# A YOCO trunk on one core: attention's pipeline started 4 modelled us later, and sixteen weight splits given to GpSimd

## Chip, core and metric

The kernel runs on one core of a Trainium2 chip. The metric is device time in microseconds (us), a median of runs. TensorE (PE in the profile; PEld is its weight load) multiplies, VectorE (DVE), ScalarE (ACT) and GpSimd (POOL) do the element-wise work, and SyncE (SP) issues most DMAs. Each engine works through its own queue in order.

## What is computed

Two layers over 1056 columns (a prompt of 1024 frames and a sample of 32), model width 1024. Layer 0 is an mLSTM mixer and a SwiGLU FFN, layer 1 a sliding-window attention and a SwiGLU FFN; each sub-layer ends in a layer norm of alpha * x + sublayer(x). The change lies in layer 1:

```python
kv = (x @ w_kv).reshape(B, T, 2, N_KV_HEADS, HEAD_DIM)
k_sh, v_sh = kv[:, :, 0], kv[:, :, 1]
...
s = jnp.einsum('bcqhgd,bckhd->bchgqk', q, k).astype(F32) * (HEAD_DIM ** -0.5) + bias
sk = sinks.astype(F32).reshape(N_KV_HEADS, GROUP)[:, :, None, None]
mx = jnp.maximum(jnp.max(s, -1, keepdims=True), sk)
p = jnp.exp(s - mx)
p = p / (jnp.sum(p, -1, keepdims=True) + jnp.exp(sk - mx))
return jnp.einsum('bchgqk,bckhd->bcqhgd', p.astype(v.dtype), v)
...
return o.reshape(B, T, D_ATT) @ w_out
```

## The kernel before

Activations lie transposed in SBUF: 128 partitions by 8 tiles of the width by 1056 columns. For projections the columns form three groups of 384, 384 and 288; for output projections and layer norms four quarters of 264. Every fp32 operand is split into a high and a low fp32r part, and each product is three matmuls, high by high, high by low and low by high (L361, L362, L363, in `gemm`). I call the three of one contraction tile a step; eight steps make an output tile.

**Weights.** The class `Weights` holds one list of units in the order of use, each 128x1024. SyncE loads a unit into one of three raw buffers `wr` (L160). A unit has two halves; for each, ScalarE copies the high part `wh` (L201) and VectorE or GpSimd subtracts to give the low part `wl` (L203). GpSimd does it unless the half is in the set `on_vector` (L314 adds output weights to it). Five slots hold split halves, and some units have homes elsewhere. `feed`, called from each step through `wv.tick`, makes the next split when a pause has passed; `mixer_out` also splits two tiles ahead in its first two quarters (`split_to`).

**Order.** `Weave` keeps generators beside the matmuls. A yielded number is a time in modelled us; each step ticks by its modelled length, and when a generator's time is up it emits its next instructions. So all queues are fixed when the program is built.

**Attention.** After layer 0, `keys_values(0)` makes keys and values of group 0 and the first four query tiles are projected. Then `v_turn` transposes the values of a group (L1668 on TensorE, L1622 and L1623 split them into `VR`; the output tag `O` has two banks, shared with the attention output), and `attention` is launched. It runs `pipeline` over 72 pairs of a two-head query tile j and a block b of 128 columns: scores (L1693, L1694 into one bank `psS` for each head, then bias and running reduction L1699 on VectorE), softmax (exponent L1711 on ScalarE, L1715 on VectorE, scaling L1717 on GpSimd), transposes of the probabilities into one bank `T` (L1737, read by L1740 on ScalarE and L1741 on VectorE, which frees it), values (L1752, L1753) and placing (L1761, L1763). Beside it run the key and value projections of groups 1 and 2 (units 108 and 109, twice), and then query projections (units 110 to 117); L1608 and L1609 on SyncE place a query tile. Later, `mixed_parts` splits attention's result (L391 on ScalarE, L392 on VectorE), and the output projection of the first quarter (units 118 to 125, `U_OUT_B[0]`, evicted at L1202) runs beside attention's last 15 steps or so. The other three quarters read the same weights again, as units 126 to 133, `U_OUT_B[1]`.

Of the kernel before, what the change touches and what calls it, by code (L numbers as in the profile page):

```python
# [101 lines left out]
def pipeline(seq, stages, order=None):  # L102


    n = [0] * len(stages)
    total = len(seq)

    def can(i):
        return n[i] < total and (i == 0 or n[i] < n[i - 1]) and stages[i][1](*seq[n[i]])

    while n[-1] < total:
        moved = False
        for i in order or range(len(stages)):
            work, _, lag, pause = stages[i]
            if not can(i) or (i + 1 < len(stages) and n[i] - n[i + 1] > stages[i + 1][2]):
                continue
            if i and n[i - 1] - n[i] <= lag and n[i - 1] < total:
                continue
            item = seq[n[i]]
            work(*item)  # L120
            n[i] += 1
            moved = True
            if pause:
                yield pause[item[0]]
        if not moved:
            yield 0.25
# [115 lines left out]
def kernel(ctx: ExitStack, tc: tile.TileContext, A, O):  # L242
# [23 lines left out]
    units, on_vector, pairs = [], set(), set()  # L266

    def add(name, idx):
        units.append(A[name][idx] if idx is not None else A[name])
        return len(units) - 1  # L270
# [15 lines left out]
    U_OUT_A = [[add("wout_a", m) for m in range(8)]] * 2  # L286
    U_UP, U_DN = [], []

    def add_ffn(layer):
        up, dn = {}, []  # L290
        for c, i in VISITS:
            held = up.get((i, 1 - c)) if i == FIRST - 1 else None
            up[i, c] = held or [add("gu", 2 * (layer * FT + i) + k) for k in range(2)]
        for i in range(FIRST, FT):
            up[i] = add_pair("gu", 2 * (layer * FT + i))
        for b in range(TAIL):
            dn.append([add_pair("dn", 4 * (layer * TAIL + b) + 2 * j) for j in range(2)])
        dn.append([add("dnt", KT * layer + m) for m in range(KT)])
        on_vector.update((u, 1) for u in dn[TAIL])
        on_vector.update((u, f) for i in range(FIRST) for c in range(2) for u in up[i, c] for f in range(2))  # L300
        U_UP.append(up)
        U_DN.append(dn)
# [8 lines left out]
    U_QB[0] += U_QB[1][4:]  # L311
    U_OUT_B = [[add("wout_b", u) for u in range(8)] for _ in range(2)]
    add_ffn(1)
    on_vector.update((u, f) for u in U_OUT_A[0] + U_OUT_B[0] + U_OUT_B[1] for f in range(2))  # L314
    on_vector.update((u, f) for u in U_Q[:1] for f in range(2))
    W = Weights(nc, base, units, pairs, on_vector)
    wv.feed = W.feed
# [1356 lines left out]
    def attention(gap):  # L1674
# [82 lines left out]
        def place(j, b):  # L1757
# [8 lines left out]
            ast["placed"] += 1  # L1766

        always = lambda j, b: True
        yield from pipeline(
            [(j, 3 * g + i) for j, g in QG for i in range(3)],  # L1770
            [
# [15 lines left out]
    wv.drain(placing)  # L1787
    wv.launch(v_turn(0, 0))
    task = wv.launch(attention((GAP_A,) * 8))
    ast["ready"] = 4  # L1790
    for g in range(1, 3):
# [179 lines left out]
```

## Time and profile before

| | us |
|---|---|
| median of 3 runs | 2244.7 (2244.04 to 2245.94) |
| the profiled execution | 2244.99 |
| its span on the core | 2242.9 |
| PE busy in the span | 2187.7 |
| DVE, ACT, POOL busy | 1472.7, 999.6, 1018.3 |

The span is the time from the profile's first instruction to its last; the rest of the execution lies around it. A row of a timeline has start, length, engine, line, operation, output and inputs by name (buffer numbers left out), shape and count, and in brackets the idle time ahead of it with what ended it. Matmul lengths overlap, so the time of one is read from start to start. A row of a stretch has bounds, length, busy time of each engine with its instructions, the granted TensorE clock (1.00 is full), the share of the DMA engines and GB/s. A row of a group ends in busy time and mean ns of one.

### The profile page before, as it was taken

To read this page: it belongs to the slowest core of one execution; us is meant where nothing else is said; L and a number is where in the kernel's file an instruction comes from. 1 tells how busy PE (TensorE), PEld (TensorE's weight loads), DVE (VectorE), ACT (ScalarE), POOL (GpSimd) and SP (SyncE) were. 2 spreads that over 40 slices of the span, in tenths; PEclk is the share of its full clock that TensorE was granted. 3 is DMA by queue.
4 is the path that set the end of the run, shared out by engine and by line. 5 is a ranking of instruction groups with operands and counts; after the bars stand their busy time and mean duration, and the time that the engine had idled before them with its cause. 6 is when DMAs were issued, how large, how long until landed. Compare 5 with 4: busy or idle time off the path is not lost.

```text
span 2242.9 us, 44249 instructions
## 1 busy us (share of the span) xinstructions
PE 2187.7 (98%) x17086; PEld 2151.6 (96%) x17086; DVE 1472.7 (66%) x2864; ACT 999.6 (45%) x2253; POOL 1018.3 (45%) x961
## 2 busy tenths in 40 slices
PE   9999999999999999999998999899999999999997
PEld 9899999999999999999998999899999999999997
DVE  4465576777566665566667678888666666456657
ACT  4443355465344444322246678656444444332124
POOL 2544331003665666545326676400566666554422
PEclk9999999999999999999999999999999999999999
DMA  4222112211443443697425433421344434397712
GB/s 149 75 54 69 53 40 86 96 39 58 165 138 140 154 152 137 230 332 232 153 79 169 115 99 95 138 78 39 106 154 160 139 134 154 135 347 242 257 50 78
DMA packets 174499, 298.10 MB, mean 133 GB/s; under 512 B 18065, under 2 KB 130761, under 8 KB 174289
## 3 DMA queue, kind: packets, MB, share of 16 engines
q1 hardware_dynamic: 169936, 290.94, 39.1%
q10 hardware_dynamic: 4352, 4.33, 0.6%
q8 instruction: 135, 2.21, 0.4%
q14 instruction: 76, 0.61, 0.1%
HBM read 201.80 MB, written 82.94 MB: 127 GB/s over the span
## 4 chain that ended last, share of the span: by engine, by line
PE 80%; DVE 8%; ACT 4%; DMA 3%; issue 3%; POOL 1%; SPq 0%; ACTq 0%; DVEq 0%; POOLq 0%
PE A L361 9%; PE A L363 9%; PE A L362 9%; PE d L361 8%; PE d L363 8%; PE d L362 8%; PE B L361 7%; PE B L362 7%; PE B L363 7%; PE T L1737 1%; DMA wr<-in_dn 1%; ACT act L463 1%; PE T L906 1%; PE O L1752 1%; DVE wl L203 1%
## 5 line engine op out<-in xcount | busy, mean ns | idle before, releaser
L203 POOL TENSOR_TENSOR wl_s<-wr,wh_s 128x512 fp32r<-128x512 f32 x224 | 316.6, 1434 | 243.0 <-ACT wh_s L201 182.6
L361 PE MATMUL d<-sx,wh 128*128 128x264 f32 (+2 forms) x1068 | 341.1, 319 | 0.7 <-DVE act L1525 0.7
L363 PE MATMUL d<-sx,wl 128*128 128x264 f32 (+2 forms) x1068 | 326.2, 305 | 1.4 <-POOL wl L203 1.4
L362 PE MATMUL d<-sx,wh 128*128 128x264 f32 (+2 forms) x1068 | 325.3, 305 | 0.1
L203 POOL TENSOR_TENSOR wl_a<-wr,wh_a 128x512 fp32r<-128x512 f32 x112 | 169.0, 1515 | 331.2 <-ACT wh_a L201 329.5
L201 ACT CAST wh_s<-wr 128x512 fp32r<-128x512 f32 x224 | 135.4, 617 | 310.9 <-DVE wr L178 279.4
L361 PE MATMUL A<-sx,wh_s 128*128 128x264 f32 x896 | 255.4, 285 | 3.5 <-ACT z L1358 3.5
L362 PE MATMUL A<-sx,wh_s 128*128 128x264 f32 x896 | 254.9, 284 | 0.0
L363 PE MATMUL A<-sx,wl_s 128*128 128x264 f32 x896 | 254.8, 284 | 0.0
L361 PEld LDWEIGHTS d<-sx,wh 128*128 128x128 f32 x1068 | 202.6, 190 | 4.3 <-ACT z L444 1.1
L363 PEld LDWEIGHTS d<-sx,wl 128*128 128x128 f32 x1068 | 201.6, 189 | 2.5 <-POOL wl L203 2.2
L362 PEld LDWEIGHTS d<-sx,wh 128*128 128x128 f32 x1068 | 202.3, 189 | 1.1 <-DVE sx L392 0.4
L363 PE MATMUL d<-sx,ex 128*128 128x264 f32 x624 | 177.7, 285 | 3.5 <-DVE ex L203 3.5
L361 PE MATMUL d<-sx,ex 128*128 128x264 f32 x624 | 180.6, 289 | 0.4 <-ACT sx L391 0.2
L203 POOL TENSOR_TENSOR wl<-wr,wh 128x512 fp32r<-128x512 f32 (+2 forms) x75 | 100.1, 1344 | 177.5 <-ACT wh L201 154.5
L362 PE MATMUL d<-sx,ex 128*128 128x264 f32 x624 | 177.3, 284 | 0.3 <-DVE sx L392 0.2
L361 PEld LDWEIGHTS A<-sx,wh_s 128*128 128x128 f32 x896 | 169.3, 189 | 4.0 <-ACT z L1358 4.0
L363 PEld LDWEIGHTS A<-sx,wl_s 128*128 128x128 f32 x896 | 169.6, 189 | 0.0
L362 PEld LDWEIGHTS A<-sx,wh_s 128*128 128x128 f32 x896 | 169.2, 189 | 0.0
L1270 POOL TENSOR_TENSOR z<-z 128x528 fp32r<-128x528 f32 x76 | 105.3, 1385 | 109.2 <-issue 58.0
L1717 POOL TENSOR_SCALAR s<-s,st 128x256 f32<-128x256 f32 (+1 forms) x144 | 126.6, 891 | 61.3 <-DVE st L1715 47.6
L1269 ACT CAST z<-z 128x528 fp32r<-128x528 f32 x136 | 85.9, 631 | 95.5 <-DVE z L1282 44.9
(338 smaller groups left out, 7299.3 us busy)
## 6 DMA issues: line engine op xcount, KB each, us to landing
wr<-in_gu SPq DMA_DIRECT2D x92, 512.0 KB, 4.9
hs_x<-z SPq DMA_DIRECT2D x72, 528.0 KB, 2.8
hs_t<-z SPq DMA_DIRECT2D x64, 528.0 KB, 2.9
sx<-hs_x SPq DMA_DIRECT2D x112, 264.0 KB, 5.9
sx<-hs_t SPq DMA_DIRECT2D x64, 264.0 KB, 6.4
ex<-hs_t SPq DMA_DIRECT2D x64, 264.0 KB, 6.4
wr<-in_dn SPq DMA_DIRECT2D x32, 512.0 KB, 3.9
ex<-hs_x SPq DMA_DIRECT2D x32, 264.0 KB, 5.9
```

Of the source, the lines that this page charges most:

```text
L201: self.nc.scalar.copy(hi, r)
L203: eng.tensor_sub(lo, r, hi.bitcast(F32))
L361: nc.tensor.matmul(out, ah, bh, start=start and k == 0, stop=False, **kw)
L362: nc.tensor.matmul(out, ah, bl, start=False, stop=False, **kw)
L363: nc.tensor.matmul(out, al, bh, start=False, stop=stop and k == last, **kw)
L463: nc.scalar.activation(z, z, AF.Identity, scale=gk, bias=bk)
L906: nc.tensor.matmul(pc[:, : 2 * (DV + 1)], keys, vt[j][:L, c], start=True, stop=True)
L1269: nc.scalar.copy(hi.bitcast(F32R), buf(s))
L1270: eng.tensor_sub(lo.bitcast(F32R), buf(s), hi)
L1717: nc.gpsimd.tensor_scalar_mul(p[:R, h, lo:256], p[:R, h, lo:256], st[:R, 2, h : h + 1])
L1737: nc.tensor.transpose(pt[:nk, i, h, :R], p[:R, h, c : c + nk], ident[:R, :R])
L1752: nc.tensor.matmul(po[:, :, :R], v, s["hi"][:nk, i, :, :R], start=(i == 0), stop=False)
```

## The change

`U_OUT_B[0]` leaves the set `on_vector`, so the low parts of the sixteen halves of units 118 to 125 are made by GpSimd. And the generator of `attention` yields 4.0 ahead of its pipeline.

```diff
-    on_vector.update((u, f) for u in U_OUT_A[0] + U_OUT_B[0] + U_OUT_B[1] for f in range(2))
+    on_vector.update((u, f) for u in U_OUT_A[0] + U_OUT_B[1] for f in range(2))
...
         always = lambda j, b: True
+        yield 4.0
         yield from pipeline(
```

On TensorE, at the start of attention (`d` is a projection, `O` here a transposed value tile, `psS` scores), before:

```order
L1668 MATMUL O_14303<-ident,act 128x128
L1693 MATMUL psS_13944<-KH_13946,Q_14111 128x128
L1694 MATMUL psS_13944<-KL_13948,Q_14111 128x128
L1693 MATMUL psS_13945<-KH_13946,Q_14111 128x128
L1694 MATMUL psS_13945<-KL_13948,Q_14111 128x128
L1693 MATMUL psS_13944<-KH_13946,Q_14111 128x256
```

And there in the changed kernel:

```order
L1668 MATMUL O_14303<-ident,act 128x128
L361 MATMUL d_14293<-sx,wh_0_14197 128x384
L362 MATMUL d_14293<-sx,wh_0_14197 128x384
L363 MATMUL d_14293<-sx,wl_0_14198 128x384
L1668 MATMUL O_14310<-ident,act 128x128
...
L1668 MATMUL O_14320<-ident,act 128x128
...
L361 MATMUL d_14342<-sx,wh_0_14261 128x384
L362 MATMUL d_14342<-sx,wh_0_14261 128x384
L363 MATMUL d_14342<-sx,wl_0_14262 128x384
L1693 MATMUL psS_13944<-KH_13946,Q_14111 128x128
```

Two blocks of scores stood right behind the first value transpose; now the rest of the key projection (`d_14293`), two more transposes and the first step of the value projection (`d_14342`) are ahead of the first scores. The twelve first attention steps move back in the same way, among the projections of group 2 and of the first queries; six value transposes now stand among them, three before. From the projection of unit 111 on, the order of TensorE is the old one.

On GpSimd, in the last part of attention (`wl` is the low part of a split, `s` the probabilities of one step):

```order
 L1717 TENSOR_SCALAR s_16964<-s_16964,st_16965 128x256 x2
+L203 TENSOR_TENSOR wl_1_17020<-wr_15495,wh_1_17019 128x512
 L1717 TENSOR_SCALAR s_17010<-s_17010,st_17011 128x256 x2
+L203 TENSOR_TENSOR wl_0_17083<-wr_15668,wh_0_17082 128x512
 L1717 TENSOR_SCALAR s_17056<-s_17056,st_17057 32x160 x2
 L1717 TENSOR_SCALAR s_17108<-s_17108,st_17109 128x256 x2
+L203 TENSOR_TENSOR wl_1_17166<-wr_15668,wh_1_17165 128x512
+L203 TENSOR_TENSOR wl_0_17172<-wr_16022,wh_0_17171 128x512
 L1717 TENSOR_SCALAR s_17150<-s_17150,st_17151 128x256 x2
 L1717 TENSOR_SCALAR s_17214<-s_17214,st_17215 128x256 x2
+L203 TENSOR_TENSOR wl_1_17274<-wr_16022,wh_1_17273 128x512
+L203 TENSOR_TENSOR wl_0_17280<-wr_17023,wh_0_17279 128x512
```

GpSimd had only scalings there; now two splits stand behind every second one. On VectorE the same splits leave a place just ahead of L1763 and L1741 (`act` is attention's result, `lo` the low part of the transposes `T`):

```order
 L1202 SCALAR_TENSOR_TENSOR act<-act,d_17175 128x264
-L203 TENSOR_TENSOR wl_1_17274<-wr_16022,wh_1_17273 128x512
-L203 TENSOR_TENSOR wl_0_17280<-wr_17023,wh_0_17279 128x512
 L1763 TENSOR_TENSOR act<-O_17246,t_17287 64x32 x2
 L1741 TENSOR_TENSOR lo_17293<-T_17291,hi_17292 128x512
```

The read of the transposes now follows the eviction of the output tile (L1202) and the placing alone.

## The prediction

> **What bounds the kernel now.** I read the page first, for what is busy and for the chain of work that ended last; then that chain in order of time over the attention stage; then the timeline of single engines at its waits.
>
> ```profile
> span 2242.9 us, 44249 instructions
> PE 2187.7 (98%) x17086; PEld 2151.6 (96%) x17086; DVE 1472.7 (66%) x2864; ACT 999.6 (45%) x2253; POOL 1018.3 (45%) x961
> PE 80%; DVE 8%; ACT 4%; DMA 3%; issue 3%; POOL 1%; SPq 0%; ACTq 0%; DVEq 0%; POOLq 0%
> 1216.80:1264.70 47.90, 41.26 (x280) 38.57 (x278) 30.76 (x112) 31.13 (x98) 35.17 (x46) 0.96 0.50 136
> 1394.00:1446.00 52.00, 44.14 (x349) 41.82 (x346) 44.88 (x152) 40.29 (x120) 29.30 (x30) 0.97 0.39 124
> ```
>
> TensorE sets the time. The last two rows are stretches (bounds, length, then busy time of PE, PEld, DVE, ACT, POOL, granted clock, DMA): the start of attention, where the delay acts, and its end, where the moved splits lie. TensorE's idle time there, 47.90 - 41.26 = 6.64 us and 52.00 - 44.14 = 7.86 us, is all that the change can win, with what a reduced clock costs there. At the end VectorE is the fullest helper, 44.88 of 52.00 us, and GpSimd has 22.70 us free.
>
> **The first edit, the 4 us ahead of the pipeline.** It adds no instruction. Eight steps of the key projection (three 384-wide matmuls each) and three value transposes come ahead of the first scores, and from the query projection of unit 111 on TensorE's order is the old one. So a delay is not carried on by the order; what can change is the idle time up to 1264.7 us.
>
> ```profile
> 1215.23 0.34 PE L361 MATMUL d<-sx,wh 128*128 128x384 f32 x1
> 1215.76 0.34 PE L361 MATMUL d<-sx,wh 128*128 128x384 f32 x1
> 1216.80 0.27 PE L1668 MATMUL O<-ident,act 128*128 128x128 f32 x1
> 1220.61 0.39 PE L1693 MATMUL psS<-KH,Q 128*128 128x256 f32 x1 [3.14 <-DVE st L1699]
> 1228.92 0.38 PE L1693 MATMUL psS<-KH,Q 128*128 128x256 f32 x1 [0.53 <-DVE st L1699]
> 1248.04 0.33 PE L1668 MATMUL O<-ident,act 128*128 128x128 f32 x1 [0.48 <-DVE VR L1623]
> 1250.01 0.35 PE L1752 MATMUL O<-hi,VR 128*128 128x256 f32 x1 [1.24 <-DVE act L1763]
> 1264.69 0.36 PE L1693 MATMUL psS<-KH,Q 128*128 128x256 f32 x1 [1.14 <-DMA Q<-qh]
> ...
> 1220.06 0.29 DVE L1623 TENSOR_TENSOR VR<-O,VR 128x128 fp32r<-128x128 f32 x1
> 1220.57 2.53 POOL L203 TENSOR_TENSOR wl<-wr,wh 128x512 fp32r<-128x512 f32 x2
> ...
> 1220.00:1222.00 2.00, 1.39 (x8) 1.14 (x8) 1.21 (x9) 0.91 (x5) 2.00 (x3) 0.88 0.98 357
> 1222.00:1224.00 2.00, 2.00 (x9) 1.70 (x8) 1.06 (x7) 1.26 (x5) 2.00 (x5) 0.50 1.09 256
> 1224.00:1226.00 2.00, 1.89 (x12) 1.56 (x12) 0.85 (x5) 0.65 (x3) 2.00 (x3) 0.77 1.00 208
> ```
>
> The number in brackets is idle time ahead of the row. A step takes 1215.76 - 1215.23 = 0.53 us.
>
> *The first wait.* The second scores wait 3.14 us: VectorE is still in the tail of the layer norm, so the bank isn't read. Now the third transpose stops instead, since its two buffers hold the first two. TensorE reaches it at 1216.80 + 3 x 0.53 + about 0.15 = 1218.55; the first buffer is read at 1220.06 + 0.29 = 1220.35. The wait is 1.8 us, a gain of 1.3. The weights behind it are in time: the split pair of the value projection ends at 1223.10 and its first half half-way, at 1221.8, while TensorE gets there at 1220.4 + 4 x 0.53 = 1222.5.
>
> *The clock.* Behind the old wait three rows show 0.88, 0.50 and 0.77: lost are 2 x (0.12 + 0.50 + 0.23) = 1.7 us.
>
> ```profile
> 1371.64 0.41 PE L1737 MATMUL T<-ident,s 128*128 128x128 f32 x2 [1.65 <-DVE st L1715]
> 1360.00:1380.00 20.00, 18.35 (x137) 17.56 (x136) 17.33 (x66) 16.00 (x52) 10.73 (x16) 1.00 0.35 101
> ...
> 1440.55 1.09 PE L1737 MATMUL T<-ident,s 128*128 128x128 f32 x4 [2.20 <-DVE lo L1741]
> 1440.00:1442.00 2.00, 1.45 (x7) 1.48 (x8) 1.11 (x5) 0.61 (x3) 1.00 (x2) 0.50 0.78 231
> 1442.00:1444.00 2.00, 2.00 (x13) 1.86 (x11) 1.41 (x4) 0.96 (x3) 0.34 (x1) 0.65 0.00 0
> ```
>
> A wait of 1.65 us left the clock at 1.00, one of 2.20 us halved it. My 1.8 us lies nearer to the first: gain 1.7, bounds 0 and 1.7. The Trainium skill's page "TensorE: Matmul & The Clock Gate", in "Why this matters for your kernels", allows gaps up to about 3 us; by that rule 1.8 us is safe and the gain 1.7 too, but the 2.20 us row was not safe, so I hold to the rows.
>
> *What comes late instead.* The first softmax runs from scores to transposes with one score bank for each head and no fill in stock; before, it ran under the slowed matmuls and cost 0.53. I put 1.6 for it, half of the 3.14 of the old start: a loss of 1.1, bounds 0 and 2.6. Further on, three value transposes among attention steps cost 0.48 + 1.24 = 1.7 us, since they share two buffers with the attention output. Now six stand among attention steps: a loss of 1.7, bounds 0 and 3.4. The wait of 1.14 us for the placed queries goes: the projection behind those queries now has attention work in it: gain 1.1, bounds 0 and 1.1.
>
> Sum: -1.3 - 1.7 + 1.1 + 1.7 - 1.1 = **-1.3 us**; the bounds give -4.1 to +3.6.
>
> **The second edit, sixteen splits to GpSimd.** VectorE loses sixteen L203, GpSimd gains them.
>
> ```profile
> L203 DVE TENSOR_TENSOR wl<-wr,wh 128x512 fp32r<-128x512 f32 x17 | 11.3, 696 | 0.0
> L203 POOL TENSOR_TENSOR wl<-wr,wh x14: 1257/1290/1306, 1247.6 to 1331.9; 128x512 fp32r<-128x512 f32 x14
> L1717 POOL TENSOR_SCALAR s<-s,st 128x256 f32<-128x256 f32 x24 | 25.9, 1093 | 18.1 <-DVE st L1715 17.5 <-PE psS L1694 0.7
> L1717 POOL TENSOR_SCALAR s<-s,st 32x160 f32<-32x160 f32 x6 | 4.0, 677 | 2.3 <-DVE st L1715 1.8 <-PE psS L1694 0.5
> ...
> 1433.64 1.83 POOL L1717 TENSOR_SCALAR s<-s,st 128x256 f32<-128x256 f32 x2 [3.53 <-DVE st L1715]
> 1437.26 2.73 POOL L1717 TENSOR_SCALAR s<-s,st 128x256 f32<-128x256 f32 x2 [1.79 <-DVE st L1715]
> ...
> 1437.91 1.27 DVE L203 TENSOR_TENSOR wl<-wr,wh 128x512 fp32r<-128x512 f32 x2
> 1439.11 0.57 DVE L1763 TENSOR_TENSOR act<-O,t 64x128 f32<-64x128 f32 x2
> 1439.72 0.69 DVE L1741 TENSOR_TENSOR lo<-T,hi 128x512 fp32r<-128x512 f32 x1
> ...
> 1413.35 0.63 PE L1737 MATMUL T<-ident,s 128*128 128x128 f32 x4 [0.75 <-DVE st L1715]
> 1419.84 0.63 PE L1737 MATMUL T<-ident,s 128*128 128x128 f32 x4 [0.61 <-DVE st L1715]
> 1426.34 0.63 PE L1737 MATMUL T<-ident,s 128*128 128x128 f32 x4 [0.76 <-DVE st L1715]
> ```
>
> VectorE is freed of 16 x 0.70 = 11 us, GpSimd takes 16 x 1.29 = 20.6 us into 22.7 free. It matters where they queue. On VectorE a pair stands ahead of L1763 and L1741, and L1741 gives back the one bank of transposes, for which TensorE waits every 6.5 us (1413.35, 1419.84, 1426.34). On GpSimd a pair stands ahead of the scaling L1717, which the same transposes need. In such a period of two attention steps GpSimd has 2 x 1.83 + 2 x 1.29 = 6.24 us of work: it becomes the pace, 0.26 us quicker than now. Over the five full periods from 1407 to 1442 that is a gain of 1.3, bounds 0 and, with all three quoted waits gone and the like in the two other periods, 5 x 0.7 = 3.5.
>
> At 1440.55 a pair of 1.27 us stood ahead of L1741, and the scaling at 1437.26 took 2.73 instead of 1.83 us beside it. Without it the wait of 2.20 falls to about 1: gain 1.2, bounds 0 and 2.2. The clock behind it lost 2 x (0.50 + 0.35) = 1.7 us; I count half, 0.9, as the neighbouring waits may add up to a long one elsewhere.
>
> Against that stands a collision.
>
> ```profile
> 1253.40 1.29 POOL L203 TENSOR_TENSOR wl<-wr,wh 128x512 fp32r<-128x512 f32 x1
> 1253.50 1.34 DVE L1623 TENSOR_TENSOR VR<-cv,VR 128x128 fp32r<-128x128 f32 x1
> L392 DVE TENSOR_TENSOR sx<-act,sx 128x384 fp32r<-128x384 f32 x8 | 4.4, 550 | 0.0
> L392 DVE TENSOR_TENSOR sx<-act,sx 128x288 fp32r<-128x288 f32 x7 | 3.1, 455 | 0.3
> ```
>
> L1623, which took 0.29 us on a PSUM operand, took 1.34 with two SBUF operands beside a split on GpSimd and ended with it. The 15 L392 of the stretch have two SBUF operands as well. GpSimd is in a split 20.6 / 52 = 40% of the time, and the mean rest of one is 0.65 us: 15 x 0.4 x 0.65 = 3.9 us for VectorE, of which I take a third on the path, since it has 11 us more room: a loss of 1.4, bounds 0 and 3.9. The splits' end: the last is needed by the last tile of the first quarter, two tiles after it is issued, and hidden; without that cover it would cost its 1.29 us.
>
> Sum: -1.3 - 1.2 - 0.9 + 1.4 = **-2.0 us**; the bounds give -7.4 to +3.9. Together -3.3 us. The profiled execution took 2244.99 us (2242.9 and 2.1 around the span), 0.3 above the median: 2241.7 there, and about 2241.5 us as a median.
>
> **Rivals.**
>
> *Both waits go in full.* No softmax start-up is left, the six transposes cost nothing, and the scaling on GpSimd, no longer stretched, keeps TensorE fed: -4.1 of the first edit and about -4.4 of the second (3.5 - 0.3, and 1.2 of the late wait): -8.5, 2236 us. For it: between 1247.6 and 1331.9 us fourteen splits ran on GpSimd beside the same scalings. Against: two SBUF operands collide, and most of those splits stood singly between scalings.
>
> *GpSimd's queue starves TensorE; slower.* A split pair holds a ready scaling for 2.58 us, as GpSimd works in order; the transposes, then all matmuls behind them, wait. It decides where less than 2.58 us lie idle ahead of the scaling: the rows show 3.53 and 1.79. If half a pair is uncovered in six periods, that is 6 x 1.3 = 7.8 us, and two waits over 2 us cost 1.7 each of clock: 11.2, less 1.3 of the first edit and 2.2 of the VectorE waits: +7.7, 2252 us.
>
> *The port takes it all.* All 3.9 us of the collision fall on the path and the delay just moves its waits: -1.3 - 1.2 - 0.9 + 3.9, and 0 for the first edit, +0.5: 2245 us. The Trainium skill, page "SBUF — State Buffer", section "Who interferes with whom", speaks against this change: a VectorE instruction with two SBUF inputs and a GpSimd one that reads SBUF exclude each other for a whole instruction. The 1.34 us row agrees; by it nearly all 15 could wait, and this rival's time would come out.
>
> **How the numbers follow.** The forecast 0.35, both waits gone 0.29, starving 0.22, the port 0.14. The range 2235.5 to 2250 us holds the first, second and last and the near part of starving. About 0.2% (4.5 us) is what a measurement of this kernel can tell from no change: the forecast lies 3.2 us below, so a part of it counts as faster, and a part of "both waits gone" as the same: faster 0.34, same 0.42, slower 0.24.
>
> **What would show it.** Right, if the 3.14 us wait is replaced by one of some 1.8 us ahead of L1668 with the clock at 1.00 behind it; if the wait for the placed queries is gone; if L1737 waits for L1717 in place of L1741 and L1715, at steps of about 6.3 us; if the 2.20 us wait and the half clock at 1440 are gone; if L392 on VectorE takes up to 1.3 us in places. Wrong, if a transpose waits over 2 us for L1717, if the clock falls behind the value transposes, or if TensorE idles more than 6.6 us up to the first scores of the next query group.

## The result and the profile after

The changed kernel takes 2236.9 us (median of 11 runs, 2235.5 to 2240.3) against 2244.7 for the kernel before on the same chip (11 runs, 2243.1 to 2246.4): 7.8 us less, a ratio of 0.9968 with a 95% interval of 0.9960 to 0.9976. It is faster by more than 0.2%. A second measurement on another chip gave 2238.6 against 2245.3: 6.7 us less, 0.9973 (0.9962 to 0.9983). The forecast of 2241.5 had the sign right and the size at less than half; the range held the time with 1.4 us to spare. The time came out where the rival "Both waits go in full" had put it.

The page of the changed kernel, and its rows of the two stretches in which the prediction looked:

```profile
span 2233.7 us, 44246 instructions
PE 2184.5 (98%) x17086; PEld 2147.9 (96%) x17086; DVE 1465.8 (66%) x2848; ACT 998.1 (45%) x2253; POOL 1035.1 (46%) x977
1216.80:1264.70 47.90, 43.98 (x307) 41.30 (x306) 31.22 (x125) 32.94 (x106) 36.40 (x48) 1.00 0.56 149
1394.00:1446.00 52.00, 46.87 (x376) 44.33 (x375) 41.94 (x136) 39.23 (x115) 39.05 (x40) 1.00 0.44 139
```

TensorE's idle time fell in the first stretch from 6.64 to 47.90 - 43.98 = 3.92 us, in the second from 7.86 to 5.13, and the clock is 1.00 in both, where it was 0.96 and 0.97. GpSimd now works 39.05 of the 52 us in place of 29.30.

To place the gain I take five marks that both programs have: 0.53 us (one step) ahead of the first value transpose, where the delay begins to act; the eviction L1601 of the first projection of unit 111, behind which the order of TensorE is the old one; the 49th and the 72nd reciprocal L1715 of attention; and the first layer norm matmul L422 behind it. Here are the last four of the kernel before:

```profile
1270.65 0.50 ACT L1601 ACTIVATE qh<-d 128x384 fp32r<-128x384 f32 x1
1367.59 0.17 DVE L1715 RECIPROCAL st<-st 128x2 f32<-128x2 f32 x1
1440.69 0.15 DVE L1715 RECIPROCAL st<-st 32x2 f32<-32x2 f32 x1
1456.10 0.38 PE L422 MATMUL ln<-z,onesm 128*128 128x264 f32 x1
```

And all five of the changed kernel:

```profile
1215.09 0.27 PE L1668 MATMUL O<-ident,act 128*128 128x128 f32 x1
1265.21 0.50 ACT L1601 ACTIVATE qh<-d 128x384 fp32r<-128x384 f32 x1
1362.53 0.17 DVE L1715 RECIPROCAL st<-st 128x2 f32<-128x2 f32 x1
1432.72 0.14 DVE L1715 RECIPROCAL st<-st 32x2 f32<-32x2 f32 x1
1447.70 0.38 PE L422 MATMUL ln<-z,onesm 128*128 128x264 f32 x1
```

| stretch | before | after | difference |
|---|---|---|---|
| start, to L1601 of unit 111 | 54.38 | 50.65 | -3.73 |
| to the 49th reciprocal | 96.94 | 97.32 | +0.38 |
| late, 49th to 72nd reciprocal | 73.10 | 70.19 | -2.91 |
| to L422 | 15.41 | 14.98 | -0.43 |
| sum | 239.83 | 233.14 | -6.69 |

So 6.7 us lie where the change acts; the +0.38 between the two gains I can't name. (In this trace the changed kernel is 1.7 us early before the first mark already, where its program is the old one, and wins another 0.8 us behind the last. Neither lies where the programs differ, so neither counts.) The start, which I took for the smaller half, gave the larger.

How well such a stretch repeats can be read from the traces of the experiments: the late stretch takes 73.02 to 73.10 us in the five with the old late order, and 70.17 to 70.33 in the eight with the new one. The start takes 54.38 and 54.60 us in the two that start as before, and 50.32 to 51.08 in the five that start as the changed kernel does.

**The start.** The waits of TensorE in it, and the clock:

```profile
1218.68 0.33 PE L1668 MATMUL O<-ident,act 128*128 128x128 f32 x1 [1.64 <-DVE VR L1623]
1223.92 0.38 PE L1693 MATMUL psS<-KH,Q 128*128 128x256 f32 x1 [0.18 <-DVE st L1699]
1239.85 0.33 PE L1668 MATMUL O<-ident,act 128*128 128x128 f32 x1 [0.47 <-DVE VR L1623]
1241.82 0.36 PE L1752 MATMUL O<-hi,VR 128*128 128x256 f32 x1 [1.25 <-DVE act L1763]
1253.15 0.38 PE L1752 MATMUL O<-hi,VR 128*128 128x256 f32 x1 [0.22 <-DVE VR L1623]
...
1218.00:1220.00 2.00, 1.32 (x8) 1.32 (x9) 1.00 (x4) 1.25 (x5) 2.00 (x2) 1.00 0.88 317
1220.00:1222.00 2.00, 2.00 (x15) 2.00 (x14) 0.34 (x1) 0.48 (x1) 2.00 (x3) 1.00 1.11 292
1222.00:1224.00 2.00, 1.82 (x12) 1.31 (x10) 1.26 (x9) 0.98 (x5) 1.27 (x4) 1.00 0.94 223
```

The third value transpose waits 1.64 us where the second scores waited 3.14. The clock stays at 1.00 behind it. The later wait for bias and reduction (L1699) is 0.18, not 0.53; none for the placed queries is left. Three more value transposes among attention steps cost 0.22 us.

What both first waits end on is the tail of the layer norm on VectorE, and in that tail stands something that the prediction doesn't name: its last L475 takes 1.80 us before (at 1217.64) and 1.83 us after (at 1215.92), beside an L475 on GpSimd, where the one just ahead of it took 0.69 and 0.70. No run here takes that 1.1 us away, so whether the two hold each other up there is not shown.

**The late part.** GpSimd from 1411 us on, then TensorE's waits:

```profile
1411.01 2.53 POOL L203 TENSOR_TENSOR wl<-wr,wh 128x512 fp32r<-128x512 f32 x2
1413.51 3.62 POOL L1717 TENSOR_SCALAR s<-s,st 128x256 f32<-128x256 f32 x4
1417.10 2.54 POOL L203 TENSOR_TENSOR wl<-wr,wh 128x512 fp32r<-128x512 f32 x2
...
1409.29 0.55 PE L1737 MATMUL T<-ident,s 128*128 128x128 f32 x3 [0.57 <-POOL s L1717]
1421.51 0.55 PE L1737 MATMUL T<-ident,s 128*128 128x128 f32 x3 [0.35 <-POOL s L1717]
1428.19 0.63 PE L1737 MATMUL T<-ident,s 128*128 128x128 f32 x4 [0.95 <-DVE lo L1741]
1432.04 0.63 PE L1737 MATMUL T<-ident,s 128*128 128x128 f32 x4 [1.44 <-DVE lo L1741]
```

From 1403 to 1425 GpSimd goes from scaling to split and back without a pause: each row begins where the one above it ends. TensorE keeps step with it: two periods last 1421.51 - 1409.29 = 12.22 us, against 12.99 between the rows of before (1413.35 to 1426.34). Then the waits for L1741 are back.

Ahead of these periods three waits of TensorE have become shorter. The first was 1.65 us before (1371.64, shown in the prediction); here are the other two, and all three of the changed kernel:

```profile
1396.23 0.63 PE L1737 MATMUL T<-ident,s 128*128 128x128 f32 x4 [1.50 <-DVE st L1715]
1406.20 0.63 PE L1737 MATMUL T<-ident,s 128*128 128x128 f32 x4 [0.96 <-DVE lo L1741]
...
1365.97 0.41 PE L1737 MATMUL T<-ident,s 128*128 128x128 f32 x2 [1.04 <-DVE st L1715]
1389.92 0.63 PE L1737 MATMUL T<-ident,s 128*128 128x128 f32 x4 [0.91 <-DVE lo L1741]
1399.25 0.63 PE L1737 MATMUL T<-ident,s 128*128 128x128 f32 x4 [0.31 <-POOL wl L203]
```

As the order of TensorE is the same in both kernels here, the starts of the same transposes tell where the time is won:

| start before | start after | wait before | wait after | gained since the row above |
|---|---|---|---|---|
| 1367.59 (49th reciprocal) | 1362.53 | | | |
| 1371.64 | 1365.97 | 1.65 | 1.04 | 0.61 |
| 1396.23 | 1389.92 | 1.50 | 0.91 | 0.64 |
| 1406.20 | 1399.25 | 0.96 | 0.31 | 0.64 |
| 1432.60 | 1424.39 | 0.40 | none | 1.26 |
| 1440.55 | 1432.04 | 2.20 | 1.44 | 0.30 |
| 1456.10 (L422) | 1447.70 | | | -0.11 |

### The profile page after: what moved, and what is told of

The parts are those of the page before. It is cut to its first block, busy times and chain, and to the rows that moved or that the text cites. A ratio compares the mean times of both kernels' runs of the same rounds, so it can differ in the third digit from the quotient of the medians.

```text
span 2233.7 us, 44246 instructions
## 1 busy us (share of the span) xinstructions
PE 2184.5 (98%) x17086; PEld 2147.9 (96%) x17086; DVE 1465.8 (66%) x2848; ACT 998.1 (45%) x2253; POOL 1035.1 (46%) x977
## 4 chain that ended last, share of the span: by engine, by line
PE 77%; DVE 9%; ACT 5%; DMA 3%; issue 3%; POOL 2%; SPq 0%; ACTq 0%; POOLq 0%; DVEq 0%
PE A L361 9%; PE A L363 9%; PE A L362 9%; PE d L361 8%; PE d L363 8%; PE d L362 8%; PE B L361 7%; PE B L362 7%; PE B L363 7%; PE T L1737 1%; ACT act L463 1%; POOL wl L203 1%; DMA sx<-hs_t 1%; DMA wr<-in_dn 1%; PE O L1752 1%
## 5 line engine op out<-in xcount | busy, mean ns | idle before, releaser
L203 POOL TENSOR_TENSOR wl<-wr,wh 128x512 fp32r<-128x512 f32 (+2 forms) x91 | 120.6, 1335 | 176.1 <-ACT wh L201 153.2
```

What stands on the lines that cost most here:

```text
L203: eng.tensor_sub(lo, r, hi.bitcast(F32))
```

## The experiments

The stretches named "start" and "late" below are those of the first table. For the kernels in which the value transposes begin four steps later, the first mark is put 2.64 us (five steps) ahead of the first transpose. All kernels of one group ran on one chip beside the kernel before. A time without a ratio is that of a single execution, and is shown for its trace.

### One edit at a time

First group, with the kernel before at 2245.2 us. The delay alone:

```diff
+        yield 4.0
         yield from pipeline(
```

> The delay alone, with all splits of the output weights left on VectorE. Theory (each edit works in its own stretch, and the gains add): the wait of 3.14 us ahead of the second scores becomes one of about 1.6 ahead of the third value transpose, the half clock behind it and the wait of 1.14 us for the placed queries go: 3.3 us faster than before. The late waits ahead of the transposes of the probabilities stay (2.20 us and a halved clock at the end of attention). Rival (the delay only moves waits, and the whole gain comes from the splits): 0 to 0.5 us faster.

2242.1 us, ratio 0.9980 (0.9967 to 0.9993). Start 50.32 us, late 73.10.

The splits alone:

```diff
-    on_vector.update((u, f) for u in U_OUT_A[0] + U_OUT_B[0] + U_OUT_B[1] for f in range(2))
+    on_vector.update((u, f) for u in U_OUT_A[0] + U_OUT_B[1] for f in range(2))
```

> The sixteen splits on GpSimd alone, attention launched without the delay. Theory (the gains add): the start of attention is as before, with its wait of 3.14 us and the half clock; in the last part GpSimd works without a pause at about 6.1 us a period: 3.3 us faster than before. Rival (the whole gain comes from the splits): 6.5 to 7.5 us faster. Rival (the two need one another, since only a late start leaves room for GpSimd): about 0.

2241.8 us, ratio 0.9984 (0.9972 to 0.9997). Start 54.60, late 70.21.

Each edit moves its own stretch and leaves the other as it was: 50.32 and 70.21 alone, 50.65 and 70.19 together. The medians add up too: 3.1 + 3.4 = 6.5 us. So neither edit feeds on the other, and each is worth about 3 us, not 1.3 and 2.0. (The medians alone are rough, 1.6 to 7.4 us and 0.7 to 6.3 by their intervals; the stretches say it more closely.)

### What the half clock at the start cost

The kernel before with eleven small matmuls into the bank of the transposes, which is not yet in use, ahead of the second scores, so that TensorE isn't idle during the long wait (they add work that nothing uses):

```diff
+            if (j, b) == (0, 0):
+                w = new(psb, "T", [P, 2, 2, P])
+                for _ in range(11):
+                    nc.tensor.matmul(w[:, 0, 0, :], onesm[:], onesm[:], start=True, stop=True)
```

> The kernel before with eleven matmuls of a constant behind the first scores; their product is read by nobody. They keep TensorE busy through most of the wait of 3.14 us, which itself ends when VectorE is out of the layer norm's tail. If the half clock behind the wait is due to the idle time, the clock stays at 1.00 there and the kernel is 1.7 us faster than before though no wait was taken away. If the clock falls for another reason, it is 0 to 0.5 us slower.

2246.6 us, ratio 1.0005 (0.9991 to 1.0018): nothing gained. The fill did what it was made for, since the row that showed 0.50 in the kernel before now shows 1.00. But other waits came or grew: 0.54 and 0.26 us ahead of the first transposes of probabilities, and the later wait for L1699 (the line numbers are four higher here; L1703 is L1699):

```profile
1222.00:1224.00 2.00, 1.93 (x12) 1.40 (x10) 1.11 (x6) 1.43 (x7) 2.00 (x4) 1.00 1.10 324
1230.72 0.38 PE L1693 MATMUL psS<-KH,Q 128*128 128x256 f32 x1 [1.80 <-DVE st L1703]
```

The kernel before waited 0.53 us there, at 1228.92. VectorE's work on the fifth scores needs the second tile of the bias, which is loaded during the pipeline. So a full clock at the start only brought TensorE earlier to these waits, and the start took 55.63 us, 1.25 more than before. The 1.7 us that I had put on the clock were no term that stands by itself.

Two kernels (second group, one execution each, kernel before at 2243.4) ask whether the bias is that wait. The kernel before with the second bias tile loaded ahead of the pipeline, and then with the fill too:

```diff
+    load_bias(1)
...
-                if ast["visit"] < len(visits):
+                if 1 < ast["visit"] < len(visits):
```

> The kernel before, with the bias table of the second query tile loaded together with that of the first, well ahead of attention. The 0.53 us wait ahead of the fifth block of scores goes; the wait of 3.14 us ahead of the second scores and the half clock behind it stay. Theory: the stretch falls from 54.4 to 53.9 us. Rival (the bias is what holds the whole start back): 51 to 52 us.

> The same, and with the eleven matmuls of a constant that keep TensorE busy in the wait of 3.14 us (their product is read by nobody). With the fill alone the clock stayed at 1.00, but the stretch was 55.6 us, since a wait of 1.80 us for the bias table took the place of the half clock. Theory (the half clock cost little by itself, because the bias table came late anyway; without either the time is won): no wait over 1 us up to the twelfth step's values but for the 0.5 and 1.24 at the value transposes, 53 to 53.8 us. Rival (the softmax chain is as late as the bias): 55 us or more.

The wait of 0.53 us is gone with the early load, and start takes 53.67 us (2244.9 in all); with the fill as well it takes 53.45 (2240.2). So that wait was the bias. In the first of the two the clock was low ahead of the start, so its first wait was 1.79 us rather than 3.14, and a second half clock, behind a wait of 1.39 us for the placed queries, lies in its start; both cloud the comparison. In the second no wait over 0.64 us is left ahead of the value transposes, and still only 0.9 us are won. A half clock of 3.41 us behind the value transposes is in that stretch, so this isn't a start at full clock either. Why the two don't give what the delay gives is argued, not shown: the 2.67 us of the fill are spent on nothing, while the projection's matmuls that the delay moves into the wait are work that has to be done anyway.

### Is the rest of the start's waiting to be won?

The changed kernel with the value transposes launched 2.2 modelled us later, so that the third doesn't wait for VectorE:

```diff
-    wv.launch(v_turn(0, 0))
+    wv.launch(v_turn(0, 2.2))
```

> The changed kernel, with the three value transposes launched 2.2 modelled us later, so that four more steps of the key projection stand ahead of the first of them. Theory (the third transpose waits 1.64 us for its buffer, which VectorE reads only at the end of the layer norm's tail, and the projection could fill that): the wait goes, 1.6 us faster than the changed kernel, about 8.3 us faster than before. Rival (the first softmax then lacks that cover, and the time is lost again between scores and transposes): as the changed kernel, 6.7 us faster than before.

2239.5 us, ratio 0.9971 (0.9958 to 0.9984), no different from the changed kernel. The 1.64 us are gone; in their place came the bias again, and a half clock further on:

```profile
1235.65 0.38 PE L1693 MATMUL psS<-KH,Q 128*128 128x256 f32 x1 [0.99 <-DVE st L1699]
1249.00:1251.00 2.00, 2.00 (x11) 2.00 (x11) 0.62 (x3) 1.16 (x5) 2.00 (x2) 0.50 0.85 309
```

Start took 51.73, in a trace that is the slowest of this kernel's 12 runs. With the bias loaded early as well (third group, kernel before at 2245.3, and the changed kernel measured again beside it):

```diff
+    load_bias(1)
...
-                if ast["visit"] < len(visits):
+                if 1 < ast["visit"] < len(visits):
...
-    wv.launch(v_turn(0, 0))
+    wv.launch(v_turn(0, 2.2))
```

> The changed kernel with the value transposes launched 2.2 modelled us later and the second bias table loaded ahead of the pipeline. Theory (the changed kernel's 1.64 us ahead of the third value transpose, and the 0.99 us for the late bias table that took its place when the values were moved alone, are both waits that can be taken away by order): neither wait is left, the start stretch takes about 49 us instead of 50.65, and the kernel is about 1.5 us faster than the changed kernel on this chip, some 8 us below the kernel before (ratio about 0.9963). Rival (a wait at the start only moves on to the next late operand): the start stretch stays at 50.5 to 52 us and the time is the changed kernel's within 0.5 us.

> The changed kernel unaltered, so that it stands beside the others on one chip. Theory: 6 to 8 us below the kernel before, ratio 0.9968 give or take 0.001. Rival (a part of the first measurement was chance): 4 us or less below, ratio 0.998 or more.

2238.4 us, ratio 0.9969 (0.9958 to 0.9981), beside 2238.6 for the changed kernel, 0.9973 (0.9962 to 0.9983). In the trace the start is down to 49.48 us (50.59 in the changed kernel of this group). The wait of the third transpose is gone, with 0.34 us for a weight in its place (1220.28), and the one for the bias is 0.15 (1222.85). So both are waits that order can take away, as the theory had it, and the trace shows 1.1 us of the 1.6. The medians can't tell 1.1 us: whether this kernel is faster than the changed one stays open.

### How long a delay

Half of it (second group) and twice of it (third group), one execution each:

```diff
-        yield 4.0
+        yield 2.0
```

> The changed kernel with a delay of 2.0 in place of 4.0: four steps of the key projection stand ahead of the first scores, not nine. From the first step of that projection to the eviction of the first query projection of unit 111 it is 54.4 us in the kernel before and 50.7 in the changed one. Theory (the first steps of attention can't go on before the bias table of the second query tile has landed, at a time that the DMA queue sets, and projection steps moved ahead of the scores fill that time): the wait for the third transpose stays at about 1.6 us, and a wait of 1.5 to 2.5 us ahead of the fifth block of scores comes in: 52 to 53 us. Rival (only the end of the layer norm's tail counts): 50.7 us as with 4.0.

2236.1 us; start 52.26, in size as forecast, but by other waits: 0.68 us for L1699, 0.49 and 0.26 ahead of the first transposes of probabilities, and 2.01 further on; none at the fifth scores, where the bias was to be late. So the start-up of the first softmax that I had priced at 1.6 us is there if too little is put ahead; with 4.0 it has enough other matmuls beside it.

```diff
-        yield 4.0
+        yield 8.0
```

> The changed kernel with 8.0 in place of 4.0 ahead of the pipeline, so that all of the key and value projections' first steps come ahead of the first scores and attention stays closer packed for longer. Theory (4.0 takes all that there is to win at the start; what is delayed further comes back as denser attention work with the same late helpers): start stretch 50 to 52 us, attention's end 0 to 3 us later than in the changed kernel, total 2236 to 2240. Rival (the more projection work ahead, the fewer waits): start stretch below 50 us and total 2235 or less.

2236.6 us; late 70.33. The start stretch took 49.28, below the 50 to 52 of the theory, and TensorE's waits in it are no smaller in sum: 1.66 + 0.32 + 1.39 + 1.19 + 0.23 = 4.79 us against 3.76 in the changed kernel. With 8.0 the order is still another than the changed kernel's at the second mark, with less attention ahead of it, so the start stretch doesn't compare. From the first mark to the 72nd reciprocal it does: 217.89 us here, 218.16 and 218.03 in the two traces of the changed kernel. The theory holds for the whole: 8.0 wins nothing that 4.0 doesn't.

### Who sets the pace late

Half of the sixteen splits on GpSimd, the other half back on VectorE (one execution, second group):

```diff
+    on_vector.update((u, 0) for u in U_OUT_B[0])
```

> The changed kernel with the first half of each of the eight units split on VectorE again and the second on GpSimd. In the changed kernel GpSimd runs without a pause through the end of attention, 6.1 us for two scalings and two splits. Theory (GpSimd is the pace there): with one split, 2 x 1.83 + 1.29 = 4.95 us of work in a period, it waits again, the matmuls of a period (5.8 us) become the pace, and the stretch from the 49th to the 72nd reciprocal of attention falls from 70.2 us to 68.5 to 69.3. Rival (VectorE's order ahead of the bank of transposes is what counts, and half of that comes back): 71.5 us, between the 73.1 of before and the 70.2.

2242.9 us; late 71.65, 1.46 more than with all sixteen moved, and half of the way back to 73.10. Here are one of the waits that GpSimd has again, VectorE ahead of the read of the transposes, and the sum of TensorE's waits (line numbers are one higher, so L1742 is L1741 and L1764 is L1763):

```profile
1417.52 2.31 POOL L1718 TENSOR_SCALAR s<-s,st 128x256 f32<-128x256 f32 x2 [1.17 <-DVE st L1716]
...
1423.99 2.03 DVE L203 TENSOR_TENSOR wl<-wr,wh 128x512 fp32r<-128x512 f32 x1
1425.94 0.57 DVE L1764 TENSOR_TENSOR act<-O,t 64x128 f32<-64x128 f32 x2
1426.55 0.69 DVE L1742 TENSOR_TENSOR lo<-T,hi 128x512 fp32r<-128x512 f32 x1
...
PE T L1738 <- DVE lo L1742: 4.2, 4, 1.9
```

GpSimd has less work than in the changed kernel, idles again, and the late part is slower. What was won came from VectorE's queue: a split ahead of L1741 holds the bank of transposes, and with two engines in splits the one on VectorE took 2.03 us here. GpSimd sets the pace only in that it is next in line, when VectorE's queue is clear.

### How far the port goes

The changed kernel with the splits of the other three quarters on GpSimd as well (one execution, third group):

```diff
-    on_vector.update((u, f) for u in U_OUT_A[0] + U_OUT_B[1] for f in range(2))
+    on_vector.update((u, f) for u in U_OUT_A[0] for f in range(2))
```

> The changed kernel with the output weights of the other three quarters split on GpSimd too. Theory (moving splits pays only where VectorE's queue stands ahead of something TensorE waits for; in the output projection of the other quarters TensorE has no waits to win): the 49th to 72nd softmax as in the changed kernel (70.2 us), and total within 2 us of it. Rival (GpSimd needs 2.58 us for a pair against some 2.75 us of matmuls a tile, so the splits come late): 2 to 4 us slower than the changed kernel, with waits of TensorE for L203 on GpSimd in the output projection.

2239.6 us; late 70.17 as expected, but then TensorE loses time in one place. VectorE, GpSimd, TensorE and the clock at the first layer norm behind attention:

```profile
1443.78 1.40 DVE L601 TENSOR_TENSOR z<-act 128x528 f32<-128x528 f32 x1
1445.21 3.38 DVE L601 TENSOR_TENSOR z<-z,act 128x528 f32<-128x528 f32 x2
1448.63 1.38 DVE L603 TENSOR_TENSOR z<-z 128x264 f32<-128x264 f32 x1
...
1440.56 4.06 POOL L203 TENSOR_TENSOR wl<-wr,wh 128x512 fp32r<-128x512 f32 x3 [0.51 <-ACT wh L201]
1444.58 10.30 POOL L203 TENSOR_TENSOR ex<-wr,ex 128x512 fp32r<-128x512 f32 x7
...
1450.16 0.68 PE L422 MATMUL ln<-z,onesm 128*128 128x264 f32 x2 [2.40 <-DVE z L603]
1452.00:1454.00 2.00, 2.00 (x11) 2.00 (x11) 0.96 (x2) 0.78 (x2) 2.00 (x3) 0.50 0.84 227
```

GpSimd is in splits without a pause from 1440 to 1455. Beside them the four sums L601 and L603 on VectorE take 1.40 + 3.38 + 1.38 = 6.16 us; in the changed kernel, where GpSimd rests there, the same four take 0.70 + 1.45 + 0.43 = 2.58. TensorE gets the result 2.40 us late and runs on at half the clock: from the 72nd reciprocal to L422 it takes 17.50 us, against 14.98. (The time of 2239.6 alone can't be told from the changed kernel's 2238.6.) Neither the theory (no waits to win or lose) nor the rival (late splits; TensorE waits for none) saw this. It is the mechanism of my rival "The port takes it all" at another place: an edit like this one can lose time by it.

## Why the prediction was right or wrong

The mechanisms were named rightly, and the signs of both sums. Three of the five terms of the first sum were mis-sized; of the second, the largest gain had no term at all. That the range held the time owes something to luck: two clock terms came true by a rule that the runs don't bear out.

**The first edit**, forecast -1.3 us, measured -3.7 in the start stretch (-4.1 in the kernel with this edit alone).

- The first wait: forecast -1.3 (3.14 to 1.8), measured -1.5 (to 1.64). Right.
- The queries: forecast -1.1, measured -1.14. Right.
- The first softmax: forecast +1.1 ("half of the 3.14"), measured 0.53 to 0.18, -0.35. This error of 1.45 us and the next of 1.48 are the largest. A wait of before that came from the layer norm's tail was taken as a measure of a softmax chain that runs without it, and the 0.53 was no softmax either: it was the second bias tile. The run with 2.0 shows the size such a start-up has: 0.68 + 0.49 + 0.26 = 1.4 us, if the matmuls that cover it are left out. I had not counted which matmuls stand between the first scores and the first transposes in the new order; the order was there to be counted.
- Six value transposes: forecast +1.7, measured +0.22. To take twice the cost because six stand where three stood treats waits as a price for each instruction. The wait comes from two buffers in a short stretch, and the three new ones meet it once, for 0.22 us.
- The clock: forecast -1.7. The rows show 1.00 as forecast. By subtraction (3.73 less 1.5, 0.35 and 1.14, and 0.22 added back) some 1.0 us is left for it; no run gives it by itself, and the fill shows why: that time was in part hidden ahead of the bias. The reason given, that 1.8 us lies nearer to a wait of 1.65 than to one of 2.20, doesn't hold in general: the wait of 1.79 us in the kernel with the early bias was followed by 0.80, 0.50 and 0.85. At the third transpose the clock stayed at 1.00 in all seven traces with a wait there, of 1.25 to 1.66 us.
- The bounds: with 0 for the queries, as their own bound allows, the upper end is +4.7, not +3.6.

**The second edit**, forecast -2.0 us, measured -2.9 in the late stretch and -0.4 behind it.

- Ahead of the periods: no term in the sum, measured -1.9 (the first three gains of the second table), the largest part. There too a split or a pair stood ahead of L1763 and L1741, at 1369.60 ahead of the first; in the changed kernel none does. (Two of the rows name L1715, which follows L1741 at once. The scaling that it releases starts at 1371.73, behind these transposes of 1371.64, so the bank is what they waited for.)
- The pace: forecast 6.24 us a period and -1.3; two periods took 12.22, 6.11 each, and the fourth gain of that table is 1.26. Right. The scalings that I took at 1.83 us a pair were right (3.62 for four); the splits take 1.27 each, not 1.29.
- The long wait: forecast 2.20 to about 1, -1.2; measured 1.44, -0.76. The wait ahead of it grew from 0.56 to 0.95 us, so only -0.30 is left of it.
- The clock behind it: 0.9 counted, half of 1.7; measured -1.3. In the kernels with the fill and with the early bias the clock stayed at 1.00 behind the same wait, and from its end to L422 they take 14.26 us where the kernel before takes 15.55. In the changed kernel it was 1.00 over the whole 52 us, but that too was chance: in two of the eight traces with its late order (the delay of 8.0, and the bias with later values) the clock fell there, for a loss of only 0.1 to 0.2 us up to L422.
- The port: forecast 3.9 us on VectorE and 1.4 on the path. It happened twice:

```profile
1423.32 2.38 DVE L392 TENSOR_TENSOR sx<-act,sx 128x384 fp32r<-128x384 f32 x1
1426.37 0.45 DVE L392 TENSOR_TENSOR sx<-act,sx 128x288 fp32r<-128x288 f32 x1
1431.80 0.99 DVE L392 TENSOR_TENSOR sx<-act,sx 128x288 fp32r<-128x288 f32 x1
...
1422.74 2.53 POOL L203 TENSOR_TENSOR wl<-wr,wh 128x512 fp32r<-128x512 f32 x2
1425.87 1.83 POOL L1717 TENSOR_SCALAR s<-s,st 128x256 f32<-128x256 f32 x2 [0.60 <-DVE st L1715]
1431.21 2.74 POOL L203 TENSOR_TENSOR wl<-wr,wh 128x512 fp32r<-128x512 f32 x2
1433.93 1.65 POOL L1717 TENSOR_SCALAR s<-s,st 32x160 f32<-32x160 f32 x2
L1717 POOL TENSOR_SCALAR s<-s,st 128x256 f32<-128x256 f32 x24 | 22.3, 940 | 5.2 <-DVE st L1715 5.2
```

The L392 at 1423.32 waited out a whole split pair, 1.8 us above its 0.55; the one at 1431.80 lost 0.5; the others ran at their old length. That is 2.4 us on VectorE, not 3.9. Behind the first of them VectorE's queue is 1.8 us late, with it the L1741 of 1427.34, and for that TensorE waits the 0.95 us at 1428.19; so at most about 1 us of it reached the path. Of the L392 from 1388 to 1446 us these two are the only ones that start within a split, and both are held. Eight start or run beside a scaling, and none of them is held (1426.37: 0.45 us, within the scaling of 1425.87). The Trainium skill's rule in "SBUF — State Buffer", "Who interferes with whom", which gave that rival its chance, is borne out where a split and a VectorE instruction with two SBUF inputs meet (1.8 us here, and all four sums in the run with all splits moved). Beside a scaling, which reads SBUF too, it is not: none of the eight was held. How many meet is the order's affair: 40% of the time in splits was not 40% of the L392.

The last row also shows a gain that I left out of the forecast's sum: without splits on VectorE a scaling takes 940 ns, where it took 1093.

**The rivals.** "GpSimd's queue starves TensorE" did happen, once and small: the small scaling of 1433.93 had its sums at 1432.72 + 0.14 = 1432.86 and stood 1.07 us behind a split pair, for which TensorE waited:

```profile
1434.98 0.24 PE L1737 MATMUL T<-ident,s 32*128 32x32 f32 x1 [0.74 <-POOL s L1717]
1435.64 0.30 PE L1737 MATMUL T<-ident,s 32*128 32x32 f32 x3 [0.41 <-POOL s L1717]
```

That is 1.15 us, where the rival asked for 7.8. From the long wait's end to L422 the changed kernel takes 15.66 us, 1.40 more than the 14.26 that the old order takes at full clock, and these two waits are most of it. Together the late terms give -1.89 - 1.26 - 0.30 - 1.29 + 1.40 = -3.34, which is what the gains of the table add up to. "Both waits go in full" had the time, though not its reasons in full: 1.64 and 1.44 us of the two waits are still there. It was right in that the start-up and the six transposes cost next to nothing.

## What to carry to other kernels

When work is moved, count in the new order which matmuls cover the chain that becomes next, rather than giving that chain the length of the wait that it replaces; and price a wait for buffers once for each place where they run short, not for each instruction. An element-wise job belongs in the queue where it holds up the least that TensorE waits for, even if that engine takes nearly twice as long for it (1.27 us against 0.70 here); count every place in the old queue where it stood ahead of something that TensorE waits for, the single ones too. This pays until that engine works without a pause beside a VectorE that needs two SBUF inputs for something due. A wait that is filled, or a clock that is restored, gains only up to the next late operand: find that one first.

## What the runs showed that I had not expected

The length of one wait doesn't decide the clock behind it. In the kernel with the delay of 2.0 this wait left it at 1.00, in every row from 1240 to 1248:

```profile
1241.52 0.38 PE L1752 MATMUL O<-hi,VR 128*128 128x256 f32 x1 [2.01 <-DVE VR L1623]
```

But a wait of 1.79 us and one of 1.39 (with 0.22 right behind it), both in the kernel with the early bias (1220.96 and 1264.00), halved it. And the same wait did now the one, now the other:

- The wait of 2.20 us ahead of the last transposes, in the five traces with the old late order: halved in three (the kernel before, the delay alone, the bias with the fill), 1.00 in two (the fill, the early bias).
- The pair of some 0.47 and 1.24 us at the value transposes, in twelve traces: halved in two (the later values, shown above, and the bias with the fill), 1.00 in ten, the changed kernel among them (rows of 1239.85 and 1241.82).
- The pair of some 0.95 and 1.44 us late in the changed order, in eight traces: halved in two.

The traces do show what these half clocks have in common. Each lasts 3.41 us, or twice that, and within one trace they start whole multiples of 3.41 us apart: in the kernel before at 1187.39, 1221.52 and 1439.97 us, that is 10.0 and 64.0 of them. So the clock seems to be set anew on a fixed grid of 3.41 us, and the same wait can fall on it in different ways. The idle time of TensorE within one such step was 1.3 to 2.5 us where the clock was halved in the next, and up to 1.8 us where it was not. Between these bounds, what decides isn't settled by these runs.
